# Neighbourhood attention's values on TensorE: high and low parts of a head side by side in one stationary operand

## The chip, the cores and the metric

The kernel runs on one core of a Trainium2 chip, in one launch. The metric is the device time of that launch in microseconds (us). Five engines of the core take part, each with its own queue, worked off strictly in order: TensorE (PE) multiplies and transposes, with its weight loads shown as PEld; VectorE (DVE) and ScalarE (ACT) do everything elementwise; SyncE (SP) issues the transfers from memory; GpSimd (POOL) does next to nothing here.

## The reference, cut to what matters

An encoder of two layers works on 256 tokens of width 1024 in float32. Each layer mixes three branches, then does cross attention to a memory and a gated feed-forward network, with a layer norm behind each of the three. One branch, `yb`, is a neighbourhood attention with 8 heads of 64 dimensions over a grid of 4 rows by 64 columns:

```
proj = x @ w_in                               # qb, kb, vb are three slices of 512 columns
sc = einsum('bhjqd,bhrjkd->bhjqrk', q, k)     # scores in the window, bias added, rest masked out
p  = softmax(sc)
yb = einsum('bhjqrk,bhrjkd->bhjqd', p, v)     # the values: this is what the change touches
merged = g0 * (ya @ w_branch[0]) + g1 * (yb @ w_branch[1]) + g2 * (yc @ w_branch[2])
```

The kernel computes the scores of all 256 by 256 token pairs of a head and masks them with a bias of -1e30 outside the window, so per head the values are one product of a 256 x 256 matrix of weights with a 256 x 64 matrix.

## The kernel before, in words

**Precision.** TensorE's quick float32 form rounds its operands, so every operand is split in two: a high part (a cast, line 276, on ACT) and a low part (the difference, line 277, on DVE). A product is then three passes into the same PSUM bank, high x high, high x low and low x high: `mm3`, lines 271 to 273.

**Weights.** All weights come in units of 128 x 1024 in the order in which they are used. SP loads a unit into one of 4 `raw` buffers, ACT and DVE split it into `hi` and `lo` (8 buffers each), and this runs 7 units ahead of the product that uses it. These 355 splits are the biggest part of the work of ACT and DVE.

**Order.** A planner (`interleave`) puts the steps of all branches in one row, with a cost and a latency for each; steps of side branches go between the weight products. A scheduler then sets each engine's order of instructions at build time from that row and from which buffers are free. On the chip each engine follows its order and waits where an operand is not there.

**Buffers.** PSUM has 3 banks `acc` for the products with weights and 5 banks `att` for attention and transposes. Tiles `t` of 128 x 512 come from a pool of 10.

**The neighbourhood branch** (`near_pair`) goes over four pairs of heads per layer, 0 to 3. For each pair: scores (lines 580 and 581), bias added and maximum taken on DVE (737 to 740), exponential on ACT (742), normalised on DVE (744 and 746), four transposes per head on TensorE (754), and their results split into high and low tiles `t` (276, 277). Then `values`: for both heads of the pair and for both halves of the 256 keys, `mm3` with a stationary operand of 128 columns of `vb`, which are both heads' 64 columns. So each head's product has 128 rows of result, of which 64 are of use: 12 matmuls of 128 x 256 per pair. The useful rows are split straight from PSUM into `yb` (two casts and two subtractions of 64 x 256). `vb` itself lies in two tiles, high and low, written by `tok_copy`.

While this runs, TensorE works on the branch before: the gates `g0` and the products of `ya` with `w0`. A gate is a product of 24 matmuls of 128 x 512 in one `acc` bank per token tile, read by a hyperbolic tangent on ACT (line 823), which frees that bank; a product is 12 such matmuls, read by DVE (line 831).

Of the kernel before, what the change touches and what calls it, by code (L numbers as in the profile page):

```python
# [22 lines left out]
ALU = mybir.AluOpType  # L23
AX = mybir.AxisListType

P = 128
# [194 lines left out]
def rd(t):  # L221
    return t.bitcast(F32)


class Encoder:
# [142 lines left out]
    def tok_copy(self, n, l, xn, tiles=None, split=False):  # L368
        def evac(i, o):
            sl = slice(512 * i, 512 * i + 512)  # L370
            if n not in self.T or self.T[n][0] != l:
                self.T[n] = (l, [self.big(F32R), self.big(F32R)] if split else self.big())
            if split:
                self.split_from(o, self.T[n][1][0][:, sl], self.T[n][1][1][:, sl])
            else:
                self.nc.scalar.copy(self.T[n][1][:, sl], o)
        return self.tok(n, l, 0, xn, evac, tiles)
# [345 lines left out]
    def near_pair(self, l, t):  # L723

        st = {"w": {}}

        def scores():
            nc = self.nc
            bias = self.bias_tiles(l, t)
            if t < 3:  # L730
                self.bias_tiles(l, t + 1)
            for j in range(2):
                ps = self.att().rearrange("p (i k) -> p i k", i=NT)
                for i in range(NT):
                    self.score(ps[:, i], self.T["qb"], self.T["kb"], j, t, i)
                b = bias[j]
                nc.vector.scalar_tensor_tensor(out=b, in0=ps, scalar=0.125, in1=b, op0=ALU.mult, op1=ALU.add)
                mx, sx = self.small(2), self.small(2)
                nc.vector.reduce_max(mx, b, axis=AX.X)
                nc.vector.tensor_scalar_mul(mx, mx, -1.0)  # L740
                for i in range(NT):
                    nc.scalar.activation(b[:, i], b[:, i], AF.Exp, bias=mx[:, i:i + 1], scale=1.0,
                                         accum_out=sx[:, i:i + 1])
                nc.vector.reciprocal(sx, sx)
                for i in range(NT):
                    nc.vector.tensor_scalar_mul(b[:, i], b[:, i], sx[:, i:i + 1])
            st["e"] = bias

        def transp(j):
            pt = self.att()  # L750
            pv = pt.rearrange("p (k t) -> p k t", k=2)
            for k in range(2):
                for i in range(NT):
                    self.nc.tensor.transpose(pv[:, k, i * P:(i + 1) * P], st["e"][j][:, i, k * P:(k + 1) * P],
                                             self.ident)
            hi, lo = self.t512(F32R), self.t512(F32R)
            self.split_from(pt, hi, lo)
            st["w"][j] = [x.rearrange("p (k t) -> p k t", k=2) for x in (hi, lo)]

        def values():  # L760
            nc = self.nc
            if ("yb", l) not in self.T:
                self.T["yb", l] = self.big_act(1)
            yb = self.T["yb", l]
            vh, vl = self.T["vb"][1]
            po = self.att().rearrange("p (j t) -> p j t", j=2)
            for j in range(2):
                for k in range(2):
                    c = slice(512 * k + t * P, 512 * k + (t + 1) * P)
                    wh, wl = st["w"][j]  # L770
                    self.mm3(po[:, j], vh[:, c], vl[:, c], wh[:, k], wl[:, k], k == 0, k == 1)
            for j in range(2):
                a = slice(64 * j, 64 * j + 64)
                self.split_from(po[a, j], yb.his[0][a, t], yb.los[0][a, t])

        yield Step(scores, 0.87, 4.0, acq=2, rel=2)
        yield Step(lambda: transp(0), 0.44, 1.4, acq=1, rel=1)
        yield Step(lambda: transp(1), 0.44, 1.8, acq=1, rel=1)
        yield Step(values, 1.3, 1.6, acq=1, rel=1)


    def conv_branch(self, l, xn):
# [487 lines left out]
```

## Time and profile before

| | |
|---|---|
| time, median of 3 runs | 1125.92 us (1124.89 to 1125.96) |
| time of the profiled execution | 1125.41 us |
| its span, first to last instruction | 1123.6 us |
| PE busy | 1098.5 us, 98% |
| DVE busy | 833.0 us, 74% |
| ACT busy | 643.8 us, 57% |
| mean DMA rate | 186 GB/s |

The median is 0.5 us above the profiled execution. Line numbers are those of the kernel before. In a timeline a row is the start in us from the span's start, the duration, the engine, the line, the operation and its tiles, and in brackets how long the engine had stood idle and who ended that. A matmul's duration reaches from its start to its modelled end, and the next one starts before that; the time that a matmul takes up on TensorE is the distance to the next start. A row with x2 or x4 holds that many instructions.

### The profile page before, as it was taken

The numbers are of one execution on the slowest core, as the hardware profiler recorded it, in microseconds if no ns is written. First come the engines' busy times: TensorE is split into PE (matmuls) and PEld (weight loads), VectorE is DVE, ScalarE is ACT, GpSimd is POOL, SyncE is SP. The second block draws the span as 40 slices with busy tenths as digits, with TensorE's granted clock in tenths as the row PEclk, the third lists the DMA queues.
The fourth block names the chain that finished last, engine by engine and source line by source line (L and its number), as shares of the span: only waits on it lengthen the run. The fifth ranks groups of instructions, "written<-read, shape, count | busy, mean of one in ns | idle before, by whom it ended". The sixth has DMA issues, their size and how long they took to land.

```text
span 1123.6 us, 17442 instructions
## 1 busy us (share of the span) xinstructions
PE 1098.5 (98%) x6700; PEld 982.5 (87%) x6700; DVE 833.0 (74%) x1300; ACT 643.8 (57%) x1060; POOL 12.4 (1%) x18
## 2 busy tenths in 40 slices
PE   9999999999999999999999999999999978999997
PEld 8899998888998988888899999888889877888886
DVE  7888888567965898885487878865777576888744
ACT  5656667445554576665355667744536436666640
POOL 0000000000000000000000000000000000000001
PEclk9999999999999999999999999999999989999999
DMA  8884436657563575666747544656746344566651
GB/s 300 284 255 145 149 133 226 187 188 243 168 205 104 174 221 188 190 190 194 263 150 232 165 148 151 200 183 197 257 149 194 131 150 150 173 189 188 195 174 37
DMA packets 60466, 208.45 MB, mean 186 GB/s; under 512 B 7008, under 2 KB 8288, under 8 KB 60384
## 3 DMA queue, kind: packets, MB, share of 16 engines
q1 hardware_dynamic: 59952, 206.83, 57.2%
q8 instruction: 52, 0.85, 0.3%
q10 hardware_dynamic: 432, 0.52, 0.1%
q14 instruction: 30, 0.25, 0.1%
HBM read 204.18 MB, written 1.05 MB: 183 GB/s over the span
## 4 chain that ended last, share of the span: by engine, by line
PE 93%; DVE 3%; ACT 1%; DMA 1%; issue 1%; SPq 0%; DVEq 0%; ACTq 0%
PE acc L271 19%; PE acc L272 19%; PE acc L273 19%; PE acc L303 12%; PE acc L301 7%; PE att L272 4%; PE att L273 4%; PE att L271 4%; PE acc L299 2%; DVE lo L277 1%; DMA raw<-in_w_dram 1%; PE att L455 1%; PE att L666 1%; PE att L581 1%; PE att L580 1%
## 5 line engine op out<-in xcount | busy, mean ns | idle before, releaser
L277 DVE TENSOR_TENSOR lo<-raw,hi 128x1024 fp32r<-128x1024 f32 x355 | 432.3, 1223 | 187.0 <-ACT hi L276 181.9
L276 ACT CAST hi<-raw 128x1024 fp32r<-128x1024 f32 x355 | 371.4, 1051 | 224.0 <-PE acc L273 75.3
L272 PE MATMUL acc<-lo,big 128*128 128x512 f32 x584 | 229.5, 393 | 0.8 <-DVE lo L277 0.8
L271 PE MATMUL acc<-hi,big 128*128 128x512 f32 x584 | 229.4, 394 | 0.0
L273 PE MATMUL acc<-hi,big 128*128 128x512 f32 x584 | 226.7, 391 | 0.0
L271 PE MATMUL acc<-big,hi 128*128 128x256 f32 x704 | 200.2, 285 | 3.2 <-ACT big L335 2.4
L273 PE MATMUL acc<-big,lo 128*128 128x256 f32 x704 | 200.5, 285 | 0.6 <-DVE lo L277 0.6
L272 PE MATMUL acc<-big,hi 128*128 128x256 f32 x704 | 199.9, 284 | 0.2 <-DVE big L277 0.2
L303 PE MATMUL acc<-big,hi 128*128 128x512 f32 x588 | 149.2, 393 | 0.0
L271 PEld LDWEIGHTS acc<-big,hi 128*128 128x128 f32 x704 | 134.7, 192 | 4.4 <-ACT big L335 2.8
L273 PEld LDWEIGHTS acc<-big,lo 128*128 128x128 f32 x704 | 134.9, 192 | 1.2 <-DVE lo L277 1.0
L272 PEld LDWEIGHTS acc<-big,hi 128*128 128x128 f32 x704 | 134.9, 192 | 0.8 <-DVE big L277 0.4
L273 PEld LDWEIGHTS acc<-hi,big 128*128 128x128 f32 x584 | 110.0, 188 | 22.8
L272 PEld LDWEIGHTS acc<-lo,big 128*128 128x128 f32 x584 | 110.3, 189 | 21.0 <-DVE lo L277 1.1
L271 PEld LDWEIGHTS acc<-hi,big 128*128 128x128 f32 x584 | 110.1, 189 | 20.1 <-ACT t L823 0.2
L303 PEld LDWEIGHTS acc<-big,hi 128*128 128x128 f32 x588 | 105.1, 189 | 18.3
L301 PEld LDWEIGHTS acc<-big,lo 128*128 128x128 f32 x672 | 91.9, 190 | 6.7 <-ACT big L276 0.2
L301 PE MATMUL acc<-big,lo 128*128 128x256 f32 x672 | 94.1, 282 | 0.0
L272 PE MATMUL att<-lo,big 128*128 128x256 f32 (+1 forms) x228 | 72.6, 319 | 0.0
L271 PE MATMUL att<-hi,big 128*128 128x256 f32 (+1 forms) x228 | 72.4, 317 | 0.0
L273 PE MATMUL att<-hi,big 128*128 128x256 f32 (+1 forms) x228 | 72.3, 318 | 0.0
L307 ACT COPY t<-acc 128x256 f32<-128x256 f32 x84 | 31.2, 372 | 65.1 <-PE acc L303 65.1
(156 smaller groups left out, 1241.0 us busy)
## 6 DMA issues: line engine op xcount, KB each, us to landing
raw<-in_w_dram SPq DMA_DIRECT2D x355, 512.0 KB, 4.2
t<-in_bias_dram SPq DMA_DIRECT2D x16, 256.0 KB, 5.7
big<-in_ln_g_dram SPq DMA_DIRECT2D x6, 512.0 KB, 5.4
big<-in_ln_b_dram SPq DMA_DIRECT2D x6, 512.0 KB, 6.2
raw<-in_memT_dram SPq DMA_DIRECT2D x6, 512.0 KB, 4.6
big<-big SPq DMA_DIRECT2D x16, 128.0 KB, 2.3
x<-in_x_dram SPq DMA_DIRECT2D x4, 256.0 KB, 7.7
t<-in_memT_dram SPq DMA_DIRECT2D x3, 256.0 KB, 6.8
```

Source lines behind the costliest of these rows:

```text
L271: mm(o, lh, rh, start=first, stop=False)
L272: mm(o, lh, rl, start=False, stop=False)
L273: self.done = mm(o, ll, rh, start=False, stop=last)
L276: return (self.nc.scalar.copy(ah, src), self.nc.vector.tensor_tensor(out=al, in0=src, in1=rd(ah), op=ALU.subtract))
L277: self.nc.vector.tensor_tensor(out=al, in0=src, in1=rd(ah), op=ALU.subtract))
L299: mm(o, hi[:, 0], xa.both(0), start=True, stop=False)
L301: mm(o[:, S:], lo[:, k], xa.hi(k), start=False, stop=False)
L303: mm(o, hi[:, k], xa.both(k), start=False, stop=k == KT - 1)
L307: self.nc.scalar.copy(dst, o[:, S:])
L455: nc.tensor.transpose(pt[:, k], self.x[i][:, (n * h + k) * P:(n * h + k + 1) * P], self.ident)
L580: self.nc.tensor.matmul(o, q[m][:, h, t], k[m][:, h], start=True, stop=False)
L581: self.nc.tensor.matmul(o, q[m][:, h, t], k[2 + m][:, h], start=False, stop=True)
```

## The change

`tok_copy` writes `vb` in another layout: one tile per half of the keys, in which each head has 128 columns, its 64 high columns and then its 64 low ones. `values` uses a head's 128 columns as one stationary operand, and passes the high weights and then the low weights over it: two passes for `mm3`'s three, 8 matmuls per pair for 12. All four products of parts are then in the result, low x low too. Rows 0 to 63 of the result belong to the high part of `vb`, rows 64 to 127 to the low part, so they must be added: ACT copies the lower rows into a new tile `y`, DVE adds the upper rows to it, and `yb` is split from `y`. The planner's cost of the step goes from 1.3 to 0.96, its latency from 1.6 to 2.4.

```diff
             if split:
-                self.split_from(o, self.T[n][1][0][:, sl], self.T[n][1][1][:, sl])
+                v = self.T[n][1][i].rearrange("p (h s d) -> p h s d", s=2, d=64)
+                self.split_from(o.rearrange("p (h d) -> p h d", d=64), v[:, :, 0], v[:, :, 1])
...
-            vh, vl = self.T["vb"][1]
             po = self.att().rearrange("p (j t) -> p j t", j=2)
             for j in range(2):
                 for k in range(2):
-                    c = slice(512 * k + t * P, 512 * k + (t + 1) * P)
-                    wh, wl = st["w"][j]
-                    self.mm3(po[:, j], vh[:, c], vl[:, c], wh[:, k], wl[:, k], k == 0, k == 1)
+                    v = self.T["vb"][1][k][:, (2 * t + j) * P:(2 * t + j + 1) * P]
+                    for s in range(2):
+                        nc.tensor.matmul(po[:, j], v, st["w"][j][s][:, k], start=k == s == 0, stop=k == s == 1)
+            y = self.t512().rearrange("p (j t) -> p j t", j=2)
+            nc.scalar.copy(y[:64], po[64:])
+            nc.vector.tensor_tensor(out=y[:64], in0=po[:64], in1=y[:64], op=ALU.add)
             for j in range(2):
                 a = slice(64 * j, 64 * j + 64)
-                self.split_from(po[a, j], yb.his[0][a, t], yb.los[0][a, t])
+                nc.scalar.copy(yb.his[0][a, t], y[:64, j])
+                nc.vector.tensor_tensor(out=yb.los[0][a, t], in0=y[:64, j], in1=rd(yb.his[0])[a, t], op=ALU.subtract)
...
-        yield Step(values, 1.3, 1.6, acq=1, rel=1)
+        yield Step(values, 0.96, 2.4, acq=1, rel=1)
```

The scheduler's order changes in the stretch of the four pairs only, alike in both layers; the order of transfers on SP is the same. In the changed kernel lines below 374 lie two further down (737 becomes 739, 746 becomes 748), and those below `values` six (823 becomes 829, 831 becomes 837); 775 is the copy of `y`, 776 the addition, 779 and 780 the split. Three places follow, all in layer 0. In the names, `t_1942` and `t_1944` are the weights of the two heads of pair 3.

The first is on DVE, from where pair 3's first head has its bias added (`t_1942`). Before:

```order
L737 SCALAR_TENSOR_TENSOR t_1942<-att_2081,t_1942 128x512
L277 TENSOR_TENSOR lo_2114<-raw_2111,hi_2113 128x1024
L277 TENSOR_TENSOR big_2037<-att_2038,big_2036 64x256
L831 SCALAR_TENSOR_TENSOR big_2123<-t_1988,acc_2022 128x512
L831 SCALAR_TENSOR_TENSOR big_2131<-t_1996,acc_2029 128x512
L739 TENSOR_REDUCE s_2087<-t_1942 128x2
L277 TENSOR_TENSOR t_2078<-att_2072,t_2077 128x512
L277 TENSOR_TENSOR lo_2145<-raw_2142,hi_2144 128x1024
L277 TENSOR_TENSOR big_2037<-att_2038,big_2036 64x256
L277 TENSOR_TENSOR big_2037<-att_2055,big_2036 64x256
L737 SCALAR_TENSOR_TENSOR t_1944<-att_2096,t_1944 128x512
```

Now:

```order
L739 SCALAR_TENSOR_TENSOR t_1942<-att_2079,t_1942 128x512
L277 TENSOR_TENSOR lo_2112<-raw_2109,hi_2111 128x1024
L776 TENSOR_TENSOR t_2047<-att_2038,t_2047 64x512
L741 TENSOR_REDUCE s_2085<-t_1942 128x2
L277 TENSOR_TENSOR lo_2143<-raw_2140,hi_2142 128x1024
L780 TENSOR_TENSOR big_2037<-t_2047,big_2036 64x256
L739 SCALAR_TENSOR_TENSOR t_1944<-att_2094,t_1944 128x512
L837 SCALAR_TENSOR_TENSOR big_2121<-t_1988,acc_2022 128x512
L742 TENSOR_SCALAR s_2085<-s_2085 128x2
L837 SCALAR_TENSOR_TENSOR big_2129<-t_1996,acc_2029 128x512
L780 TENSOR_TENSOR big_2037<-t_2047,big_2036 64x256
L776 TENSOR_TENSOR t_2063<-att_2054,t_2063 64x512
```

Two additions of 64 x 512 (line 776, pairs 0 and 1) have come in between; the subtractions for `yb` (`big_2037`) now read the tile `t` in place of PSUM.

The second is on DVE too, where pair 3's weights are normalised (`t_1942`, then `t_1944`). Before:

```order
L746 TENSOR_SCALAR t_1942<-t_1942,s_2088 128x256 x2
L277 TENSOR_TENSOR lo_2253<-raw_2250,hi_2252 128x1024
L744 RECIPROCAL s_2103<-s_2103 128x2
L277 TENSOR_TENSOR lo_2275<-raw_2272,hi_2274 128x1024
L277 TENSOR_TENSOR big_2037<-att_2162,big_2036 64x256
L746 TENSOR_SCALAR t_1944<-t_1944,s_2103 128x256 x2
L277 TENSOR_TENSOR t_2185<-att_2179,t_2184 128x512
L277 TENSOR_TENSOR big_2037<-att_2162,big_2036 64x256
L277 TENSOR_TENSOR t_2212<-att_2206,t_2211 128x512
```

Now:

```order
L748 TENSOR_SCALAR t_1942<-t_1942,s_2086 128x256 x2
L277 TENSOR_TENSOR lo_2215<-raw_2212,hi_2214 128x1024
L277 TENSOR_TENSOR lo_2249<-raw_2246,hi_2248 128x1024
L746 RECIPROCAL s_2101<-s_2101 128x2
L277 TENSOR_TENSOR lo_2271<-raw_2268,hi_2270 128x1024
L776 TENSOR_TENSOR t_2169<-att_2160,t_2169 64x512
L748 TENSOR_SCALAR t_1944<-t_1944,s_2101 128x256 x2
L277 TENSOR_TENSOR t_2182<-att_2176,t_2181 128x512
L780 TENSOR_TENSOR big_2037<-t_2169,big_2036 64x256 x2
L277 TENSOR_TENSOR t_2209<-att_2203,t_2208 128x512
```

Pair 2's addition stands ahead of the second head's normalisation, and both of pair 2's subtractions, of which one stood ahead of it, stand between the two low parts of pair 3 (`t_2182`, `t_2209`).

The third is on ACT at the same time: `t_2211` (now `t_2208`) is the high part of pair 3's second head, and the line of the tangent reads the gates' banks `acc`. Before:

```order
L276 CAST big_2036<-att_2162 64x256
L276 CAST t_2184<-att_2179 128x512
L276 CAST big_2036<-att_2162 64x256
L276 CAST t_2211<-att_2206 128x512
L823 ACTIVATE t_2262<-acc_2148 128x512
L823 ACTIVATE t_2270<-acc_2155 128x512
```

Now:

```order
L775 COPY t_2169<-att_2160 64x512
L276 CAST t_2181<-att_2176 128x512
L779 CAST big_2036<-t_2169 64x256 x2
L276 CAST t_2208<-att_2203 128x512
L775 COPY t_2239<-att_2230 64x512
L829 ACTIVATE t_2258<-acc_2146 128x512
L829 ACTIVATE t_2266<-acc_2153 128x512
```

Pair 3's copy of `y` (`t_2239`, from its values' bank `att_2230`) now stands ahead of the two tangents. On TensorE, too, pair 3's values stood in two pieces, 7 matmuls, then 12 of the product of `ya`, then 5 more; now all 8 stand in one piece ahead of those 12. The amount of other work ahead of pair 3's transposes is the same in both orders.

## The prediction

> **What bounds the kernel now.** I read the page's head first, then the waits of TensorE, then the busy time of each engine in the stretch that the change touches, and last the timelines of PE, DVE and ACT there.
>
> ```profile
> span 1123.6 us, 17442 instructions
> PE 1098.5 (98%) x6700; PEld 982.5 (87%) x6700; DVE 833.0 (74%) x1300; ACT 643.8 (57%) x1060; POOL 12.4 (1%) x18
> ```
>
> Over the whole span TensorE is the bound, and a change that takes matmuls away should pay. But these are averages. Here is the stretch of pair 3 in layer 0, what follows it, and the same stretch in layer 1 (columns: window, its length, PE, PEld, DVE, ACT and POOL busy, granted clock, DMA share, GB/s):
>
> ```profile
> 175.60:190.30 14.70, 14.70 (x78) 12.45 (x78) 14.53 (x26) 9.69 (x20) 0.00 (x0) 1.00 0.64 198
> 192.00:206.00 14.00, 13.74 (x65) 11.61 (x66) 8.08 (x11) 7.37 (x10) 0.00 (x0) 1.00 0.52 164
> 716.00:730.80 14.80, 14.67 (x79) 12.28 (x77) 14.64 (x27) 9.99 (x22) 0.00 (x0) 1.00 0.58 185
> ```
>
> In these 14.7 us DVE is busy 14.53: as full as TensorE, while 74% is its mean. Behind it DVE falls to 8.08 of 14.00. And of the few waits that TensorE has in the whole kernel, three sit exactly there:
>
> ```profile
> PEld acc L271 <- ACT t L823: 0.2, 1, 0.2
> ...
> PE att L754 <- DVE t L746: 0.5, 1, 0.5
> ...
> PE att L272 <- DVE t L277: 0.3, 1, 0.3
> ```
>
> The transposes of pair 3 (754) wait for the normalisation on DVE (746), the values for a low part (277), and the next product for a gate's tangent on ACT (823), which frees its bank. So at pair 3 DVE and ACT already end last, if only by tenths of a microsecond.
>
> **What the change takes from TensorE.** Four pairs in two layers lose 4 matmuls each, 32 in all. Their price is the distance between starts:
>
> ```profile
> 195.67 0.39 PE L273 MATMUL acc<-hi,big 128*128 128x512 f32 x1
> 195.89 0.28 PE L272 MATMUL att<-t,big 128*128 128x256 f32 x1
> 196.01 0.28 PE L273 MATMUL att<-t,big 128*128 128x256 f32 x1
> ```
>
> A row says 0.28 us, but the next one starts after 0.12 (a 128x512 takes 0.22). So 32 x 0.12 = 3.8 us come off TensorE, not 9. The Trainium skill, "TensorE: Matmul & The Clock Gate", section "Back-to-back issue gap", gives for a sustained stream about 81 ns at 128 columns and 131 at 512, which by an estimate between them is some 98 ns at 256, so 3.1 us. The rows are 20% above that at 256 and 70% at 512, and the measurement decides.
>
> TensorE does not wait in this stretch (14.70 busy of 14.70), so by pair 3's transposes three pairs' savings, 12 x 0.12 = 1.4 us, have brought it forward:
>
> ```profile
> 190.20 1.26 PE L754 MATMUL att<-ident,t 128*128 128x128 f32 x8
> 193.07 0.47 PE L271 MATMUL acc<-hi,big 128*128 128x512 f32 x1
> ```
>
> It reaches them at 190.20 - 1.4 = 188.8. What counts is whether DVE is there.
>
> **What it adds to DVE.** Per pair one addition of 64 x 512; the subtractions stay, from SBUF now. The trace has no addition of that shape from PSUM and SBUF, but a subtraction of just this shape and these memories, and the copy that ACT adds:
>
> ```profile
> L570 DVE TENSOR_TENSOR big<-acc,big 64x512 fp32r<-64x512 f32 x8 | 5.5, 686 | 0.2
> ...
> L565 ACT CAST big<-acc 64x512 fp32r<-64x512 f32 x8 | 4.7, 583 | 3.0 <-DVE big L570 2.8
> ```
>
> On DVE too the step is what counts when instructions follow each other closely:
>
> ```profile
> 175.61 0.69 DVE L737 SCALAR_TENSOR_TENSOR t<-att,t 128x512 f32<-128x512 f32 x1
> ...
> 177.35 0.41 DVE L277 TENSOR_TENSOR big<-att,big 64x256 fp32r<-64x256 f32 x1
> 177.69 1.27 DVE L831 SCALAR_TENSOR_TENSOR big<-t,acc 128x512 f32<-128x512 f32 x2
> 178.88 0.67 DVE L739 TENSOR_REDUCE s<-t 128x2 f32<-128x512 f32 x1
> 179.48 0.67 DVE L277 TENSOR_TENSOR t<-att,t 128x512 fp32r<-128x512 f32 x1
> ...
> 185.21 0.43 DVE L277 TENSOR_TENSOR big<-att,big 64x256 fp32r<-64x256 f32 x1
> 185.67 0.17 DVE L744 RECIPROCAL s<-s 128x2 f32<-128x2 f32 x1
> ...
> 190.26 0.60 DVE L746 TENSOR_SCALAR t<-t,s 128x256 f32<-128x256 f32 x2
> ```
>
> From 178.88 to 179.48 a step over 512 columns takes 0.60, at most its 0.69; a subtraction of 64 x 256 takes 0.34 to 0.46 (177.35 to 177.69, 185.21 to 185.67). Call S the start of the normalisation of pair 3's second head, 190.26 here. In the new order three additions (pairs 0 to 2) stand between the bias of pair 3's first head and S, and four subtractions in place of five; all else is the same set of instructions, six weight splits among them. So S moves by 3 x 0.60 - 0.46 = 1.3 us at least and 3 x 0.69 - 0.34 = 1.7 at most. I take 1.4, near the lower end because the steps here are mostly the close ones. Nothing lets DVE start earlier: the bias add at 175.61 stands behind a weight split that TensorE's saving doesn't hasten. I went through what each instruction there waits for: ACT is busy 9.69 of 14.70, so with three copies of 0.58 more it still keeps ahead of DVE. One wait is new on TensorE, some 0.6 us before pair 2's values (the high part of pair 2's first head stands behind a copy of `y` now), and it is hidden: TensorE only reaches S less early.
>
> **What stands behind S.** S is at 191.7, TensorE is there at 189.4 at the latest, and stands still. Then a chain runs to the next product's first matmul. Its durations are best read in layer 1, where S is 730.73:
>
> ```profile
> 731.21 0.72 PE L754 MATMUL att<-ident,t 128*128 128x128 f32 x4 [0.53 <-DVE t L746]
> ...
> 732.13 0.38 PE L272 MATMUL att<-t,big 128*128 128x256 f32 x1
> 732.35 0.28 PE L273 MATMUL att<-t,big 128*128 128x256 f32 x1
> 732.47 0.28 PE L271 MATMUL att<-t,big 128*128 128x256 f32 x1
> ...
> 733.10 0.50 PE L271 MATMUL acc<-hi,big 128*128 128x512 f32 x1
> ```
>
> ```profile
> 730.73 0.60 DVE L746 TENSOR_SCALAR t<-t,s 128x256 f32<-128x256 f32 x2
> 731.38 0.69 DVE L277 TENSOR_TENSOR t<-att,t 128x512 fp32r<-128x512 f32 x1
> 732.11 0.43 DVE L277 TENSOR_TENSOR big<-att,big 64x256 fp32r<-64x256 f32 x1
> 732.58 0.69 DVE L277 TENSOR_TENSOR t<-att,t 128x512 fp32r<-128x512 f32 x1
> ```
>
> ```profile
> 731.96 0.59 ACT L276 CAST t<-att 128x512 fp32r<-128x512 f32 x1 [0.22 <-PE att L754]
> 732.44 1.09 ACT L823 ACTIVATE t<-acc 128x512 f32<-128x512 f32 x2
> ```
>
> Before, the path is S, transposes until 731.93, high part until 732.55, tangent until 733.04, next product at 733.10: S + 2.37. The low part of the second head (732.58) isn't on it, since the five matmuls behind that product use it, and these take 5 x 0.12 = 0.6 us more; with them the same work is done at S + 2.97. In layer 0 the product starts at 193.07 = S + 2.81, with the five at S + 3.41.
>
> Now all eight matmuls stand ahead, and the tangent stands behind the copy of pair 3's `y`, which needs the last of them. From S: normalisation 0.60; first low part until 1.34; two subtractions, 0.46 each, until 2.3; second low part until 3.0; three matmuls, the first after a wait, starts at 3.05, 3.27 and 3.39 (the steps at 732.13), end at 3.67; copy 0.58, until 4.3; tangent 0.60, until 4.85; next product at S + 4.9. That the high part comes at 2.07 hides. The bounds: 4.6 if copy and tangent overlap like the two tangents at 732.44 (1.09 for two of 0.60) and the subtractions step by 0.40, 5.1 if nothing overlaps.
>
> **The sum.** Per layer the time from the old position to the new one is 1.4 + 4.9 - 3.4 = 2.9 us in layer 0 and 1.4 + 4.9 - 3.0 = 3.3 in layer 1, together 6.2 us slower, and the 3.8 saved are in that: TensorE spends them waiting. By the bounds it is 1.3 + 4.6 - 3.4 and 1.3 + 4.6 - 3.0, so 5.4, to 1.7 + 5.1 - 3.4 and 1.7 + 5.1 - 3.0, so 7.2. What follows has room (DVE 8.08 of 14.00), the weights are split 7 units ahead, and nothing in the rest of the layer runs on a clock of its own that would swallow a late TensorE. The second reader, the product of `yb`, stands behind a whole gate. The rest costs nothing: `vb` written with gaps is 4 instructions on each of ACT and DVE, off the path, and copies with and without gaps cost alike:
>
> ```profile
> L276 ACT CAST big<-acc 128x512 fp32r<-128x512 f32 x20 | 11.5, 590 | 2.1 <-PE acc L273 2.1
> ...
> L857 ACT ACTIVATE big<-att 128x512 fp32r<-128x512 f32 x8 | 4.8, 598 | 3.8 <-PE att L855 3.8
> ```
>
> The profiled execution took 1125.41 us, 1.8 more than its span and 0.5 less than the median of the runs. On it 6.2 makes 1131.6, and 1130.8 to 1132.6 by the bounds.
>
> **Rivals.** First, the saving arrives: TensorE is the bound at 98%, DVE makes room, and 3.8 us come off, 1121.6. By the 3.1 of the Trainium skill it would be 1122.3. It needs S at 188.8, so DVE 2.9 us faster than I find it in a stretch where it is busy 14.53 of 14.70. I give it 8%.
>
> Second, no change: S doesn't move, since the additions fill gaps of DVE that I take for busy, and the copy of `y` costs the tangent nothing, so the product starts at S + 3.5; that is 0.1 in layer 0 and 0.5 in layer 1, 1126.0. The order on ACT speaks against the second half of it. 9%.
>
> Third, one of the two delays only: DVE is 1.4 late, but the tail is S + 3.5, or the tail is full and S is not late. That is 0.6 + 2 x 1.4 = 3.4, or 6.2 - 2.8 = 3.4: 1128.8. 15%.
>
> Fourth, more than the sum: TensorE's clock falls in the gap. After the pause of over 4 us at the last layer norms it did:
>
> ```profile
> 916.00:920.00 4.00, 0.00 (x0) 0.00 (x0) 4.00 (x7) 0.52 (x2) 0.00 (x0) 0.81 0.66 200
> 920.00:924.00 4.00, 2.44 (x12) 2.47 (x13) 4.00 (x13) 0.67 (x2) 0.00 (x0) 0.50 0.52 199
> 924.00:928.00 4.00, 4.00 (x24) 3.64 (x24) 2.82 (x8) 1.65 (x4) 0.00 (x0) 0.84 0.00 0
> ```
>
> Half the clock for 4 us and 0.84 for 4 more lose 4 x 0.5 + 4 x 0.16 = 2.6 us of work: 1134.2 if it happens in one layer, 1136.8 in both. The pause here is shorter, 189.4 to 192.1, and then come single matmuls until 196.6. The same page of the Trainium skill, section "What's actually happening", has the clock halved after one idle window of about 3.4 us, so a pause this short would not do it unless almost idle counts as idle; the trace shows the drop behind a longer pause only, and none here shows the border. I give it 10%, half of that for one layer.
>
> **How the numbers follow.** My own sum has what is left, 58%: 1131.6. The range leaves out the saving (8%) and the clock's fall in both layers (5%), and takes in no change, at 1126.0, to one layer with the clock's fall, 1134.2, and some for both ends: 1125.8 to 1135.0. A measurement of this kernel can tell about 0.2%, 2.3 us. Faster by more is the first rival and little else, 0.09; within it lies the second and a part of the third, 0.13; slower 0.78.
>
> **What would show it.** In the profile after: PE waits at pair 3's transposes for 748 by about 2 us and at the next product for 829 by about 1 us, in both layers, where 0.5 and 0.2 stood; S 1.3 to 1.7 us later after the bias of pair 3's first head than the 14.65 of before; DVE without a gap until S. Wrong would be: no wait of TensorE over 1 us there (then the first two rivals), or a granted clock under 1.00 between 185 and 205 us.

## The result, and the profile after

The changed kernel takes 1133.63 us (median of four runs, 1132.27 to 1136.29) where the kernel before takes 1125.62 beside it: the ratio is 1.0073, with an interval of 1.0061 to 1.0086. The profiled execution took 1132.27 us, 1.8 more than its span. The head of its page and the waits of TensorE (us in total, how many, the longest):

```profile
span 1130.5 us, 17401 instructions
...
PE 1098.2 (97%) x6668; PEld 980.1 (87%) x6668; DVE 837.7 (74%) x1308; ACT 649.6 (57%) x1068; POOL 12.4 (1%) x18
```

```profile
PE acc L271 <- ACT t L829: 2.6, 2, 1.3
...
PE att L756 <- DVE t L748: 1.7, 2, 0.9
PE acc L271 <- DVE big L837: 1.6, 2, 0.8
...
PE att L773 <- DVE t L277: 0.9, 2, 0.4
...
PE att L773 <- ACT t L276: 0.4, 2, 0.2
```

The 32 matmuls are gone (6668 for 6700), and the span is 6.9 us longer. Where before one wait of 0.5, one of 0.3 and one of 0.2 stood at pair 3, five kinds of wait stand now, each once in each layer. The same stretches as before, and the 2 us slices between 194 and 202 us:

```profile
175.60:190.30 14.70, 13.72 (x69) 11.24 (x68) 14.57 (x26) 10.95 (x22) 0.00 (x0) 1.00 0.57 174
192.00:206.00 14.00, 12.15 (x49) 9.53 (x49) 8.11 (x13) 6.45 (x10) 0.00 (x0) 0.88 0.42 131
194.00:196.00 2.00, 0.63 (x3) 0.42 (x3) 0.67 (x2) 1.14 (x3) 0.00 (x0) 0.94 0.41 166
196.00:198.00 2.00, 1.90 (x5) 1.54 (x6) 1.61 (x4) 1.22 (x4) 0.00 (x0) 0.50 0.00 0
198.00:200.00 2.00, 2.00 (x8) 1.63 (x7) 0.00 (x0) 0.94 (x1) 0.00 (x0) 0.71 0.00 0
...
716.00:730.80 14.80, 13.82 (x72) 11.45 (x71) 14.46 (x24) 11.43 (x20) 0.00 (x0) 1.00 0.59 198
```

TensorE now has a gap in the stretch where it had none (13.72 busy of 14.70), while DVE is as full as it was. In layer 0 the granted clock then falls to half (0.50 from 196 us on); in layer 1 it stays at 1.00 until 742 us. The instructions themselves, layer 0, TensorE, DVE and ACT:

```profile
181.17 0.50 PE L271 MATMUL acc<-hi,big 128*128 128x512 f32 x1 [0.79 <-DVE big L837]
...
190.34 0.60 PE L756 MATMUL att<-ident,t 128*128 128x128 f32 x4
191.81 0.33 PE L756 MATMUL att<-ident,t 128*128 128x128 f32 x1 [0.87 <-DVE t L748]
...
194.18 0.63 PE L773 MATMUL att<-t,big 128*128 128x256 f32 x3 [0.44 <-DVE t L277]
196.10 0.80 PE L271 MATMUL acc<-hi,big 128*128 128x512 f32 x1 [1.29 <-ACT t L829]
196.69 0.63 PE L272 MATMUL acc<-lo,big 128*128 128x512 f32 x1
197.12 0.63 PE L273 MATMUL acc<-hi,big 128*128 128x512 f32 x1
...
199.21 0.39 PE L272 MATMUL acc<-lo,big 128*128 128x512 f32 x1
199.44 0.39 PE L273 MATMUL acc<-hi,big 128*128 128x512 f32 x1
```

```profile
175.44 0.69 DVE L739 SCALAR_TENSOR_TENSOR t<-att,t 128x512 f32<-128x512 f32 x1 [0.22 <-PE att L583]
...
190.82 0.68 DVE L776 TENSOR_TENSOR t<-att,t 64x512 f32<-64x512 f32 x1
191.42 0.60 DVE L748 TENSOR_SCALAR t<-t,s 128x256 f32<-128x256 f32 x2
```

```profile
194.84 0.58 ACT L775 COPY t<-att 64x512 f32<-64x512 f32 x1 [1.54 <-PE att L773]
195.45 1.08 ACT L829 ACTIVATE t<-acc 128x512 f32<-128x512 f32 x2
```

S, the normalisation of pair 3's second head, is at 191.42, 15.98 behind the bias add at 175.44 (14.65 before); pair 2's addition stands straight ahead of it. The next product starts at 196.10, S + 4.68 (S + 2.81 before); the tangent at 195.45 stands behind the copy at 194.84, and that behind the last of the eight matmuls.

How much later the same matmul stands than in the trace of before can be read at any place of the program. The table has, for this kernel and for those of the experiments, the middle of that difference over all matmuls that both traces have, between 60 and 158 us, and from there how it grows over layer 0's stretch (to 215 and on), over layer 1's (600 to 760 and on) and over the last layer norms (900 to 940 and on). The first column lies ahead of anything that was edited and differs from trace to trace. One execution each of the kernel before, adds_only, urgent_y1 and nomax_before took 1823 us or more; the medians count these, the ratios leave them out.

| kernel | ahead of it | layer 0 | layer 1 | last norms | median of the runs |
|---|---|---|---|---|---|
| changed kernel | +0.11 | +3.81 | +2.16 | +0.77 | 1133.63 |
| adds_only | +0.27 | +5.57 | +2.90 | +0.75 | 1135.44 |
| mm_only | +0.47 | -0.91 | -1.08 | +0.06 | 1124.34 |
| late3 | +0.09 | +0.50 | +1.87 | +0.53 | 1128.47 |
| warm | +0.75 | +2.37 | +2.91 | +0.07 | 1131.41 |
| y1 | +0.20 | -0.19 | -0.36 | +0.25 | 1125.71 |
| late | +0.33 | +0.11 | +0.58 | -0.20 | 1127.13 |
| urgent_y1 | +2.06 | -0.84 | -0.76 | +0.17 | 1125.91 |
| urgent_before | +0.52 | +4.01 | +0.07 | -0.13 | 1130.32 |
| nomax_before_2 | +1.54 | -1.18 | -1.38 | -0.14 | 1123.91 |
| nomax_after | +0.95 | -1.20 | -1.40 | +0.34 | 1123.87 |
| nomax_y1 | +0.11 | -3.09 | -3.26 | +0.26 | 1119.15 |

So 6.0 of the 6.9 us are in the two stretches of pair 3. Of layer 0's 3.81 the clock has 1.5: seven steps from 196.10 to 199.21 take 3.11 us and would take 7 x 0.23 (199.21 to 199.44) = 1.6; 2.3 are waits.

### The profile page after: what moved, and what is told of

Read it like the earlier page. It is cut to its first block, busy times and chain, and to the rows that moved or that the text cites. A ratio compares the mean times of both kernels' runs of the same rounds, so it can differ in the third digit from the quotient of the medians.

```text
span 1130.5 us, 17401 instructions
## 1 busy us (share of the span) xinstructions
PE 1098.2 (97%) x6668; PEld 980.1 (87%) x6668; DVE 837.7 (74%) x1308; ACT 649.6 (57%) x1068; POOL 12.4 (1%) x18
## 4 chain that ended last, share of the span: by engine, by line
PE 90%; DVE 5%; ACT 2%; issue 1%; DMA 1%; SPq 0%; DVEq 0%; ACTq 0%
PE acc L271 18%; PE acc L272 18%; PE acc L273 18%; PE acc L303 12%; PE acc L301 7%; PE att L272 4%; PE att L273 4%; PE att L271 4%; PE acc L299 2%; DVE lo L277 1%; PE att L457 1%; PE att L668 1%; DMA raw<-in_w_dram 1%; DMA t<-in_memT_dram 1%; PE att L583 1%
```

## The experiments

The theory: DVE, full until S, and ACT, with the copy ahead of the tangent, make TensorE wait for more than the matmuls save. The kernel before ran at 1126.2 us beside all the experiments but the last, and at 1125.8 beside that one.

**One half of the change alone.** Adds_only is the kernel before with the copy and the addition added, and nobody reads their result:

```diff
+            y = self.t512().rearrange("p (j t) -> p j t", j=2)
+            nc.scalar.copy(y[:64], po[64:])
+            nc.vector.tensor_tensor(out=y[:64], in0=po[:64], in1=y[:64], op=ALU.add)
```

> The kernel before, with its twelve matmuls per pair and its old layout, plus the copy of 64 x 512 on ACT and the addition of 64 x 512 on DVE per pair, whose result nothing reads. Theory (DVE full up to S, then the copy ahead of the tangent): the additions alone bring the whole loss, since what TensorE does less is spent waiting. S about 1.3 us later in both layers, the next product at S + 4.7, so 5 to 7 us over the kernel before, about 1131.5, as the changed kernel without its clock losses; TensorE waits over 1 us for the tangent. Rival (TensorE is the bound and the matmuls are worth 3.8 us): either the additions hide and it takes 1126, or they cost the changed kernel's loss plus the 3.8 us, 1136 to 1138.

Mm_only is the changed kernel without them: `yb` is split from the upper 64 rows, and the part that belongs to the low half of `vb` is left out.

```diff
-            y = self.t512().rearrange("p (j t) -> p j t", j=2)
-            nc.scalar.copy(y[:64], po[64:])
-            nc.vector.tensor_tensor(out=y[:64], in0=po[:64], in1=y[:64], op=ALU.add)
...
-                nc.scalar.copy(yb.his[0][a, t], y[:64, j])
-                nc.vector.tensor_tensor(out=yb.los[0][a, t], in0=y[:64, j], in1=rd(yb.his[0])[a, t], op=ALU.subtract)
+                nc.scalar.copy(yb.his[0][a, t], po[:64, j])
+                nc.vector.tensor_tensor(out=yb.los[0][a, t], in0=po[:64, j], in1=rd(yb.his[0])[a, t], op=ALU.subtract)
```

> The changed kernel without the copy and the addition: yb is split from the upper 64 rows of the result alone, so the low part of vb is left out. This is the saving of 32 matmuls by itself. Theory: TensorE reaches pair 3 1.4 us earlier and waits for DVE there, since S is where it was; what arrives is the rest, 1 to 2 us in all, 1123.6 to 1124.6. Rival (TensorE is the bound): 32 x 0.12 = 3.8 us, 1121.8.

Adds_only took 1135.44 us, ratio 1.0074 (1.0057 to 1.0090): the additions alone cost no less than the whole change (the two intervals overlap). That is some 9 us over the kernel before, where 5 to 7 were expected. The clock fell here too: nine steps from 197.54 to 201.55 in layer 0 take 4.01 us and would take 9 x 0.23 = 2.07. Without those 1.94 the 5.57 and 2.90 of the two layers come to 6.53. Mm_only took 1124.34, 0.9986 (0.9977 to 0.9995): the 3.8 us of matmuls alone bring 1.9, as expected. The waits of TensorE, first of adds_only, then of mm_only:

```profile
PE acc L271 <- ACT t L826: 2.7, 2, 1.4
PE att L754 <- DVE t L746: 2.5, 2, 1.2
```

```profile
PE att L756 <- DVE t L748: 1.5, 4, 0.4
...
PE att L773 <- DVE t L277: 1.0, 2, 0.5
```

In adds_only they are the two waits of the changed kernel, for the tangent and for the normalisation. In mm_only the tangent is gone from the list, but the waits for DVE at pair 3 come to 2.5 us where they were 0.8: about half of what the matmuls save is waited away even with no addition at all. S shows why. In mm_only, layer 0:

```profile
175.81 0.69 DVE L739 SCALAR_TENSOR_TENSOR t<-att,t 128x512 f32<-128x512 f32 x1
...
190.43 0.62 DVE L748 TENSOR_SCALAR t<-t,s 128x256 f32<-128x256 f32 x2
```

It is 14.62 behind the bias add, as before: DVE sets it, and fewer matmuls don't move it. In adds_only it is 16.24 behind (175.88 to 192.12).

**The tail alone.** Late3 is the changed kernel with pair 3's copy, addition and splits in a step of their own, later; ahead of S nothing changes, but the tangents stand ahead of the copy.

```diff
+            st["po"] = po
+            if t < 3:
+                evac()
+
+        def evac():
+            nc, po, yb = self.nc, st["po"], self.T["yb", l]
...
-        yield Step(values, 0.96, 2.4, acq=1, rel=1)
+        if t < 3:
+            yield Step(values, 0.96, 2.4, acq=1, rel=1)
+            return
+        yield Step(values, 0.96, 2.4, acq=1)
+        yield Step(evac, 0, 2.4, rel=1)
```

> The changed kernel, but for pair 3 alone the copy, the addition and the split are a step of their own that comes later in the planner's row; on ACT the two tangents then stand ahead of that copy, and three of pair 3's eight matmuls stand behind the next product; all ahead of S is as in the changed kernel. Theory: the copy in the way is the bigger part. S stays 1.3 us late, but the next product starts at S + 2.7 in place of S + 4.7; less three matmuls behind it, 1.65 us per layer, 3.3 in both, and the clock does not fall in so short a pause (1.4 us in the profile of the changed kernel): 1127.2 to 1129.0, 2 to 3 over the kernel before. Rival (the additions on DVE cost it all): no less than 1131.

It took 1128.47, 1.0018 (1.0009 to 1.0028), 5.2 us under the changed kernel. Its waits of TensorE, and its slices in layer 1:

```profile
PE att L756 <- DVE t L748: 1.8, 2, 0.9
PE acc L271 <- DVE big L847: 1.6, 2, 0.8
```

```profile
730.00:732.00 2.00, 1.32 (x8) 0.87 (x6) 2.00 (x5) 0.65 (x2) 0.00 (x0) 1.00 0.87 258
732.00:734.00 2.00, 1.68 (x9) 1.16 (x9) 1.94 (x6) 1.63 (x4) 0.00 (x0) 1.00 1.00 311
734.00:736.00 2.00, 1.88 (x5) 1.43 (x5) 1.11 (x2) 0.68 (x2) 0.00 (x0) 0.58 0.51 207
736.00:738.00 2.00, 2.00 (x7) 1.51 (x6) 0.00 (x0) 0.85 (x1) 0.00 (x0) 0.56 0.00 0
```

The wait for the tangent is gone, the wait for the normalisation stays as it was. In layer 0, where the clock held, +0.50 is left of 2.3; in layer 1 the clock fell here too, and that makes most of the +1.87. The time lies in the expected range by two misses that cancel: 1.65 was expected in each layer, and no fall of the clock. So the copy ahead of the tangent, with the matmuls that it waits for, is the larger of the two delays.

**The clock.** Warm is the changed kernel with two groups of five 128 x 128 matmuls at pair 3 that nobody reads, ahead of the second head's transposes and behind the values.

```diff
+            if t == 3 and j == 1:
+                for _ in range(5):
+                    self.nc.tensor.matmul(pt[:, :P], self.ident, self.ident, start=True, stop=True)
...
+            if t == 3:
+                self.warm(5, mm)
```

> The changed kernel with two times five small matmuls on the identity, whose results nothing reads, in pair 3: ahead of its second head's transposes and behind its values. The orders of ACT and DVE are as in the changed kernel. Theory of the clock: TensorE's pauses at pair 3 are long enough for its clock to fall in some executions, which is 1.4 us in layer 0 of the profile and the spread of the four times (1132.3 to 1136.3). With the small matmuls in the pauses the granted clock is 1.00 from 185 to 205 us and in layer 1, and all times lie within 1 us at 1130.5 to 1131.5. Rival (the spread is something else): same times and spread as the changed kernel, or later by the small matmuls, about 1 us per layer.

It took 1131.41, 1.0047 (1.0032 to 1.0062), 2.2 us under the changed kernel with ten matmuls more in each layer. The 12 us around pair 3 in both layers:

```profile
186.00:198.00 12.00, 11.31 (x68) 9.45 (x67) 10.43 (x21) 8.15 (x17) 0.00 (x0) 1.00 0.55 175
...
726.00:738.00 12.00, 11.46 (x63) 9.50 (x63) 11.63 (x22) 8.28 (x15) 0.00 (x0) 1.00 0.52 181
```

The clock holds in both (0.91 in the first of these windows in the changed kernel), and layer 0 loses 2.37 for 3.81. The waits themselves stay, filled by the added matmuls. The expectation of four times within 1 us missed: they run from 1130.54 to 1133.11. The four runs of the changed kernel agree: the two of about 1132.3 us had a mean granted clock of 0.993 and 0.994, the one of 1134.85 had 0.991, and the one of 1136.29 had 0.988.

**The order mended.** Y1 is the changed kernel with `y` in a buffer of its own; nothing else is edited, and the scheduler then puts two additions ahead of S and the tangents ahead of the copy. Late has the late step of late3 for all four pairs.

```diff
-            y = self.t512().rearrange("p (j t) -> p j t", j=2)
+            y = self.tmp.tile([P, 512], F32, tag="y", name=self.nm("y"), bufs=1).rearrange("p (j t) -> p j t", j=2)
```

```diff
+            st["po"] = po
+
+        def evac():
+            nc, po, yb = self.nc, st["po"], self.T["yb", l]
...
-        yield Step(values, 0.96, 2.4, acq=1, rel=1)
+        yield Step(values, 0.96, 2.4, acq=1)
+        yield Step(evac, 0, 2.4, rel=1)
```

> The changed kernel with y in a buffer of its own; that alone alters the order: two additions instead of three stand ahead of S on VectorE, one weight split fewer stands there, the gate's tangents stand ahead of pair 3's copy on ScalarE, and one of pair 3's eight matmuls stands ahead of the next product. Theory (the loss is a matter of what stands ahead of S and ahead of the tangent): S is at most 0.5 us later after the bias of pair 3's first head than the 14.65 of before, TensorE's wait for the tangent is under 0.5 us, and the time is 1124 to 1126.5. Rival (VectorE's and ScalarE's added work costs wherever it stands): 1129 or more. Rival (the clock's fall makes the loss, and any pause at pair 3 brings it): granted clock under 0.95 from 185 to 205 us and 1128 or more.

> The changed kernel with the copy, addition and splits of y one step later for all four pairs, so that two additions stand ahead of S and the tangents ahead of pair 3's copy. Theory: S about 0.6 us less late than in the changed kernel (1.33 late there), no wait for the tangent over 0.5 us: 1125 to 1127.5. If the copy ahead of the tangent were all of the loss, it would be as late3 gave, 1128.5; if the additions' work costs wherever it stands, 1129 or more.

Y1 took 1125.71, ratio 0.9998 (0.9988 to 1.0007), and late 1127.13, 1.0012 (1.0001 to 1.0023). The loss is gone with the order alone, which speaks against the rival that the added work costs wherever it stands. In late the tangent's wait is gone, but S, at 191.31, is hardly earlier than the 191.42 of the changed kernel. It is 13.32 behind its bias add, but that add itself has moved back in the order, to 177.99. Its four waits for a normalisation come to 4.1 us, and the 0.6 that was expected of S is missing; the time is in the expected range, but not by an earlier S. In y1 S is 14.40 behind the bias add (175.53 to 189.93), even earlier than before. But y1 gains nothing. Two waits of TensorE in its layer 0:

```profile
181.86 0.50 PE L271 MATMUL acc<-hi,big 128*128 128x512 f32 x1 [0.90 <-DVE big L837]
...
192.77 0.49 PE L271 MATMUL acc<-hi,big 128*128 128x512 f32 x1 [1.06 <-ACT t L829]
```

Together they are 1.96 us, and the matmuls save 16 x 0.12 = 1.92 in a layer. The expectation of under 0.5 for the tangent missed: as in the kernel before, the tangent stands behind the high part of the second head on ACT, and that behind the transposes, but only one of pair 3's matmuls is left ahead of the next product to fill that time, where there were seven.

**DVE's order ahead of S.** Urgent_y1 is y1, urgent_before the kernel before, each with the normalisations set ahead of the weight splits.

```diff
-                    nc.vector.tensor_scalar_mul(b[:, i], b[:, i], sx[:, i:i + 1])
+                    self.urgent(nc.vector.tensor_scalar_mul(b[:, i], b[:, i], sx[:, i:i + 1]))
```

> y1 and, besides, the normalisation of each pair set ahead of the weight splits on VectorE. Theory (VectorE's queue ahead of S is what eats the saving): TensorE no longer waits for the normalisation of pair 3 (under 0.2 us in both layers), and the saving of 32 matmuls of 0.12 us arrives: 1121.5 to 1123.5. Rival (the weight splits, put behind, are then late for the next products): a wait of TensorE for a weight's high or low part in place of it, 1125 or more.

> The kernel before with the normalisation of each pair set ahead of the weight splits on VectorE, nothing else; it tells what of urgent_y1's time is that order alone. Theory: TensorE hardly waits in the kernel before (0.5 us for the normalisation, 0.3 for a low part), so at most 0.5 to 1 us comes off: 1125 to 1126. Rival (the order itself is worth the time): 1123 or less.

Urgent_y1 took 1125.91, 0.9996 (0.9987 to 1.0006): the rival was right, though by another route than it named. Its DVE in layer 0, and TensorE:

```profile
187.24 0.62 DVE L748 TENSOR_SCALAR t<-t,s 128x256 f32<-128x256 f32 x2
187.77 4.62 DVE L277 TENSOR_TENSOR lo<-raw,hi 128x1024 fp32r<-128x1024 f32 x4
```

```profile
193.99 0.50 PE L271 MATMUL acc<-hi,big 128*128 128x512 f32 x1 [2.00 <-ACT t L829]
```

S is 4 us earlier than in the changed kernel (187.24, 9.09 behind its bias add), and no wait for it is left; but the weight splits stand in a block of 4.62 us behind it, and TensorE waits 2.00 for the tangent. Urgent_before, which was to be a little faster, took 1130.32, 1.0036 (1.0022 to 1.0049): TensorE waits 2.00 there too, the clock falls (0.91 from 185 to 205 us), and layer 0 alone loses 4.01. Set ahead in this way, the normalisation leaves DVE the same load at another place; what remained to be tried is less load.

**DVE's load.** In the last kernels the softmax of neighbourhood attention doesn't subtract the row maximum, so 0.84 us of DVE's work per head is left out; in exact arithmetic the quotient is the same without it.

```diff
-                mx, sx = self.small(2), self.small(2)
-                nc.vector.reduce_max(mx, b, axis=AX.X)
-                nc.vector.tensor_scalar_mul(mx, mx, -1.0)
+                sx = self.small(2)
                 for i in range(NT):
-                    nc.scalar.activation(b[:, i], b[:, i], AF.Exp, bias=mx[:, i:i + 1], scale=1.0,
-                                         accum_out=sx[:, i:i + 1])
+                    nc.scalar.activation(b[:, i], b[:, i], AF.Exp, scale=1.0, accum_out=sx[:, i:i + 1])
```

> The kernel before, whose softmax of neighbourhood attention doesn't subtract the row maximum: for each of eight heads in a layer a reduction of 0.67 us and a small product of 0.17 are left out of VectorE's work, some 4 us of them ahead of S. It is the base for the two kernels after it. TensorE hardly waits at pair 3 in the kernel before, so with the same matmuls little can come off: 1124.5 to 1126.5; slower by up to 4 if the weight splits bunch as they did in urgent_before.

> The changed kernel with the same left out. Theory (the changed kernel loses because VectorE, full until S, makes TensorE wait): no wait of TensorE for a normalisation (under 0.2 us in both layers), and 3 to 6 us less than the changed kernel's 1133.6; what stays of the loss is the tangent behind pair 3's copy. Rival (the loss doesn't hang on VectorE's load): within 1.5 us of 1133.6.

> y1 with the same left out: VectorE has room and the tangents stand ahead of the copy, so neither of the two delays is left. Theory: the saving of 32 matmuls arrives, 2.5 to 3.8 us under nomax_before: 1121 to 1123. Rival (the weight splits, bunched behind the normalisations, are late in place of it): TensorE waits over 1.5 us at pair 3 in each layer and the time is 1125 or more.

> The same kernel as nomax_before, for a profile of it: nomax_y1 came 4.8 us under it, 1.0 more than the 3.8 of the 32 matmuls. Theory: the 1.0 is what TensorE waits in this kernel at pair 3, some 0.5 us in each layer for the tangent or a low part, and not in nomax_y1. Rival: no wait there, then a matmul saved is worth more than 0.12 us or another place gives it.

The kernel before so edited took 1123.98 us, and 1123.91 in the second run, from which its profile is (0.9980, 0.9970 to 0.9990). The changed kernel took 1123.87 (0.9981, 0.9972 to 0.9990), 9.8 less than without the edit, and y1 1119.15 (0.9943, 0.9931 to 0.9956). That is 0.57% under the kernel before, and the fastest here. TensorE's waits in nomax_after at this place, one row:

```profile
PE acc L271 <- ACT t L826: 2.7, 2, 1.3
```

The wait for the normalisation is gone. The clock holds (1.00 from 185 to 205 us), which is a part of why more came off than the 3 to 6 us expected: 1.5 us in layer 0 of the changed kernel's trace. The wait for the tangent behind the copy stays, up to 1.3 in each layer, and by the table nothing of the 1.9 is left over nomax_before. In nomax_y1 this wait is gone too. Its bias add of pair 3's first head and its S:

```profile
175.60 0.68 DVE L739 SCALAR_TENSOR_TENSOR t<-att,t 128x512 f32<-128x512 f32 x1
...
180.86 0.61 DVE L745 TENSOR_SCALAR t<-t,s 128x256 f32<-128x256 f32 x2
```

S is 5.26 behind the bias add, where it was 14.40 in y1, and what is left out of DVE's work doesn't account for so much. The edit changes the order too: no weight split stands between the two now, where five stood in y1 and six in the kernel before. Urgent_y1 has none there either, and all of the load, and it gained nothing. So moving the splits isn't enough by itself, which speaks for the load; but no run takes the load off and keeps the order. The windows from 185 and from 725 us, first of nomax_y1, then of nomax_before_2:

```profile
185.00:205.00 20.00, 20.00 (x97) 16.81 (x96) 14.71 (x18) 12.64 (x19) 0.00 (x0) 1.00 0.65 209
...
725.00:746.00 21.00, 21.00 (x96) 17.44 (x95) 14.15 (x18) 11.30 (x16) 0.00 (x0) 1.00 0.67 207
```

```profile
185.00:205.00 20.00, 20.00 (x102) 17.01 (x101) 13.97 (x16) 11.12 (x16) 0.00 (x0) 1.00 0.57 173
...
725.00:746.00 21.00, 21.00 (x107) 17.83 (x106) 13.65 (x16) 12.17 (x17) 0.00 (x0) 1.00 0.60 188
```

By these windows TensorE doesn't wait in either, so between these two the saving must show in full: layer 0 goes from -1.18 to -3.09 and layer 1 from -1.38 to -3.26, 1.91 and 1.88, together 3.8, which is 32 x 0.12. The expectation that the remaining 1.0 of the 4.8 was a wait at pair 3 in nomax_before fell: it has none. In the profiled executions 1.4 lie ahead of the edited stretches (+1.54 and +0.11 in the table). Whether that holds for the medians too, and why, stays open.

## Why the prediction was right, and where it was not

**The saving.** Right in its size: 3.8 us, seen where nothing waits. Right, too, that the change as it stands spends it waiting. The 128 x 512 steps at the full clock are 0.23 (199.21 to 199.44) and at half 0.43 (196.69 to 197.12). The Trainium skill has two sets of figures for this on the page "TensorE: Matmul & The Clock Gate": the section "Wait — 56ns, not 53.3ns?" gives 215.7 ns and 426.7 at 512 columns, which these rows nearly bear out, and the sustained 131 of "Back-to-back issue gap", which the prediction weighed, is not seen here.

**S.** Predicted 1.3 to 1.7 later, taken 1.4; it is 1.33 later in layer 0 (15.98 for 14.65). In layer 1 the bias add is at 719.16 and S at 735.14:

```profile
719.16 0.69 DVE L739 SCALAR_TENSOR_TENSOR t<-att,t 128x512 f32<-128x512 f32 x1 [0.21 <-PE att L583]
...
735.14 0.60 DVE L748 TENSOR_SCALAR t<-t,s 128x256 f32<-128x256 f32 x2
```

That is 15.98 again, for 14.64 (716.09 to 730.73). Three additions more and one subtraction less ahead of it was the whole account.

**The tail.** Predicted S + 4.9, with bounds of 4.6 and 5.1; it is S + 4.68 in layer 0 and, by the product at 739.81, S + 4.67 in layer 1. The subtractions step closely and copy and tangent overlap, so it lies near the lower bound. The wait for the tangent was to be about 1 us and is 1.29. That it comes of the copy's place on ACT is what late3 shows, where it is gone.

**TensorE's arrival.** It was to be at the transposes at 189.4 and to wait 2 us. It comes to the first head's at 190.34 and waits 0.87 for the second's. The one new wait that the step named, 0.6 ahead of pair 2's values, is there with 0.19. The step missed another: at 181.17 the product of `ya` waits 0.79 for line 837, which frees its bank and which the additions have pushed back on DVE. It costs nothing, since TensorE would have waited for S instead.

**The sum.** For layer 0 2.9 was predicted, and the waits came to 2.3. The terms measured, 1.33 + 4.68 - 3.41, make 2.6; the rest is that the bias add came earlier than before: by 0.17, and by 0.28 when the 0.11 by which the whole trace lies behind there is taken off. For layer 1 3.3 was predicted and 2.16 measured. The failing step is "Nothing lets DVE start earlier: the bias add at 175.61 stands behind a weight split that TensorE's saving doesn't hasten". In the kernel before, weights came late ahead of this stretch, on ACT and so on DVE:

```profile
713.87 1.05 ACT L276 CAST hi<-raw 128x1024 fp32r<-128x1024 f32 x1 [1.30 <-DMA raw<-in_w_dram]
```

```profile
714.95 1.23 DVE L277 TENSOR_TENSOR lo<-raw,hi 128x1024 fp32r<-128x1024 f32 x1 [1.01 <-ACT hi L276]
```

Neither wait is in the changed kernel, where the bias add waits for TensorE's scores instead (0.21 in the row at 719.16). TensorE comes to layer 1 3.93 late (0.11 + 3.81 + 0.01), the bias add is only 3.07 late (719.16 for 716.09), and 0.86 come off: 1.33 + 4.67 - 2.97 - 0.86 = 2.17. It isn't TensorE's lateness that hides the wait: in y1 TensorE comes to layer 1 0.02 late, and the bias add, at 715.25, is 0.84 earlier than before. In warm DVE still waits for a weight there:

```profile
717.94 1.22 DVE L277 TENSOR_TENSOR lo<-raw,hi 128x1024 fp32r<-128x1024 f32 x1 [0.93 <-ACT hi L276]
```

Its bias add, at 719.08, is 2.99 late for TensorE's 3.13, and layer 1 loses 2.91, much nearer to the 3.3. By these traces the weights make the difference; why they come late in some traces and in time in others stays open.

**The clock.** A granted clock under 1.00 between 185 and 205 us was named as a sign of being wrong, and it was 0.91. The fourth rival, at 10%, took the clock's fall as coming on top of the whole sum; it came on top of less, in layer 0 of the profiled execution with 1.5 us for the 2.6 that it named, and by the granted clocks of 0.991 and 0.988 with more in two other runs. So the total came out near partly by luck: the waits made 2.3 + 2.2 = 4.5 of the 6.2 forecast, and the clock and the last norms, whose 0.77 no run here explains, filled the rest and more in the median, 1133.63 for 1131.6. The other rivals fell: the saving doesn't arrive, S and the tail are both late, and TensorE waits more than 1 us.

## What to carry to other kernels

A saving on the busiest engine is worth what that engine doesn't then wait in the stretch where it is saved; read the window of that stretch for a second engine that is as full, and count what stands ahead of the one instruction that the first will wait for. A short copy out of PSUM that is added to a queue costs by what stands behind it there: the same copy, ahead of a tangent or behind it, with three matmuls that moved along, was worth 5 us, the clock's fall behind it included. Where two engines are full, take load off the second one first: 0.84 us per head, with the order that the scheduler made of it, let the saving on the first come in whole.

## What the runs showed of the hardware

The granted clock fell to half without any long pause. In late3's layer 1 the longest single wait of TensorE ahead of it was 0.89 us:

```profile
732.20 0.33 PE L756 MATMUL att<-ident,t 128*128 128x128 f32 x1 [0.89 <-DVE t L748]
```

By the slices above TensorE was busy 3.00 of the 4 us from 730 to 734, and the clock was 0.58 in the next two. In the changed kernel nearly the same sequence of waits (0.87, 0.44, 1.29) halved the clock in layer 0 and left it alone in layer 1. So several short waits can do what the one long pause at the last norms does, and not each time; and longer waits need not do it: in urgent_y1 waits of 2.00 and 2.23 us left the clock at 1.00 in both layers. No rule for the border comes out of these traces. The Trainium skill, "TensorE: Matmul & The Clock Gate", section "What's actually happening", has the clock fall after an idle window of some 3.4 us, from a window that runs freely; section "A second HAM failure mode: psum-queue depth-cycling" has short idle times between groups of matmuls doing it. The traces agree with the second, and the chance from one layer to the next would fit a window that runs freely; no run here tests that. With ten small matmuls in the gaps the clock was 1.00 in both layers of the one trace of warm.
